# Products with stationary weights: three 256-column matmuls into one accumulator instead of a 512- and a 256-column one that are joined

## The chip, the core and the metric

The kernel runs on one core of one Trainium2 chip. The metric is the device time of one execution in microseconds. TensorE multiplies and writes to accumulators in PSUM; VectorE, ScalarE and GpSimd do the elementwise work; SyncE and ScalarE issue the DMAs. The engines run side by side and wait for one another through semaphores.

## The reference, cut to what matters

One layer of a decoder, for 256 tokens of width 2048, in float32:

```
h   = rmsnorm(x, mix_norm_g)
qkv = h @ w_in                       # 2048 x 6144: 8 + 8 heads of 128, each q, k, v
a   = softmax attention on heads 0-7 (q and k rotated in 32 of 128 dimensions, causal)
b   = stick-breaking attention on heads 8-15 (sigmoids and running products, causal)
x   = x + concat(rmsnorm(a, moba_out_g), rmsnorm(b, sb_out_g)) @ w_out
u   = rmsnorm(x, mlp_norm_g) @ w_up  # 2048 x 8192
x   = x + square(relu(u)) @ w_down   # 8192 x 2048
out = rmsnorm(x, final_norm_g)
```

With 256 tokens there is one block of keys, so the block selection of the first group selects nothing more than its own block.

## The kernel before, in words

Weights of 201 MB are streamed from HBM in 192 items of 1 MiB (512 rows x 512 columns), 48 for q, k and v, 16 for the output projection, 64 for the up and 64 for the down projection. `fetch` (L101) issues an item three items ahead on SyncE's queue into one of three buffers. ScalarE and VectorE split each item into two float32r parts, `wh` (L117, the rounded value) and `wl` (L123, the rest). Activations are split into hi and lo in the same way, and lie side by side in one tile: `actT[:, kt, 0:256]` is hi, `actT[:, kt, 256:512]` is lo. A product is then the sum of three: hi with wh, hi with wl, and lo with wh.

Two forms of product exist. `x_stationary` and `x_part` (L235 to L254) put the tokens on the partitions: activations are loaded as weights of the array, and 512 columns of the weights stream through it, in three matmuls (L242, L243, L244). It serves v, the output and the down projection. `w_stationary` (L218) puts the columns of the weights on the partitions, and the 256 tokens stream: q, k and the up projection, 32 + 64 = 96 items. An item has 4 column blocks (m) and 4 row blocks (k), so 16 steps, and each step of before has two matmuls: L227 loads wh and streams hi and lo, 512 columns, into the two halves of an accumulator; L228 loads wl and streams hi, 256 columns, into the second half. The first half then holds hi*wh, the second hi*wl + lo*wh. Four items (j) complete an accumulation, and at the last step of a block `done(m)` is called.

For q and k, `done` leads to `head_out` (L403) and `qk_out` (L302): ScalarE copies the second half into `low` (L305), VectorE adds the first to it (L306). At a slot of the schedule, `qk_scale` (L308) rotates the first 32 rows if the head is of the first group (L312 to L315, VectorE) and multiplies all by the row scale `r1b` of the first norm (L316, GpSimd). For the up projection, `done` leads to `up_out` (L467): copy of the second half on ScalarE (L471), add on VectorE (L472), maximum with zero times itself (L473), then the split of the result into hi (L474, ScalarE) and lo (L475, GpSimd).

There are six accumulators of 512 columns (`acc`) and two for attention (`att`). A group of q, k or up blocks uses four of the six.

The order of the work on each engine is written out by hand: `step` (L268) runs one item, with the split of the item two ahead woven in, and `at(slot, f)` puts attention and scaling work into slots, two of them in an item. The row scale `r1b` is made at slot 12, in item 6; the first q heads are complete after item 3, the first k heads after item 11.

Of the kernel before, what the change touches and what calls it, by code (L numbers as in the profile page):

```python
# [9 lines left out]
F32 = mybir.dt.float32  # L10
F32R = mybir.dt.float32r
AF = mybir.ActivationFunctionType
ALU = mybir.AluOpType
AX = mybir.AxisListType

P = 128
S = 256
# [6 lines left out]
HALF = 16  # L24
# [7 lines left out]


def shape_constants():
    """What depends on shapes alone: the rotary angles and the causal mask's fill."""
    inv = (THETA ** (-np.arange(HALF, dtype=np.float32) / HALF)).astype(np.float32)
    ang = np.arange(S, dtype=np.float32)[None, :] * inv[:, None]
    c, s = np.cos(ang, dtype=np.float32), np.sin(ang, dtype=np.float32)
    out = np.zeros((P, 2 * S + 3 * P), np.float32)
    out[:2 * HALF, :S] = np.concatenate([c, c])  # L40
    out[:2 * HALF, S:2 * S] = np.concatenate([-s, s])
    diag = np.where(np.arange(P)[None, :] <= np.arange(P)[:, None], 0.0, NEG)
    out[:, 2 * S:2 * S + P] = diag
    out[:, 2 * S + 2 * P:] = diag
    return out
# [3 lines left out]
def layer(ctx: ExitStack, tc, x, mix_g, w_in, moba_g, sb_g, w_out, mlp_g, w_up, w_down, fin_g,  # L49
          consts, out):  # L50
    nc = tc.nc
# [5 lines left out]
    att = pool("att", 2, space=bass.MemoryType.PSUM)  # L57
    ctx.enter_context(tc.manual_schedule())

    # ---- constants and small operands  # L60
    xs = cp.tile([P, 2, D], F32, name="xs")
    xv = x.rearrange("(t p) d -> p t d", p=P)
    grow = cp.tile([2 * HALF, P], F32, name="grow")
# [2 lines left out]
    cosr, sinr, dmask = cst[:32, :S], cst[:32, S:2 * S], cst[:, 2 * S:]  # L66

    def load_x(c):
# [7 lines left out]
                            fill=0.0, base=0, channel_multiplier=1)  # L76
    mhalf = cp.tile([P, 2], F32, name="mhalf")
    nc.gpsimd.memset(mhalf, -0.5)

    # ---- weight stream: 1 MiB items, each split exactly into two float32r parts  # L80
    items = []
    for h in range(2):
        for kind in ("q", "v", "k"):
# [15 lines left out]
    raws, parts = {}, {}  # L99
# [26 lines left out]
        split_hi(i, slice(k, k + n))  # L126
        split_lo(i, slice(k, k + n))

    # ---- row statistics
    def rms_scale(r, ss, n):  # L130
        """r = (ss / n + eps) ** -0.5"""
        nc.vector.tensor_scalar(r, ss, 1.0 / n, EPS, op0=ALU.mult, op1=ALU.add)
        nc.gpsimd.tensor_tensor(r, r, mhalf[:, :r.shape[-1]], op=ALU.pow)

# [2 lines left out]
    actT = cp.tile([P, 16, 2 * S], F32R, name="actT")  # L137

    def to_columns(src, gcol, kts, between=None):
        """Transposes [token, d] into d on the partitions, times gain, in two parts."""  # L140
        ps = [att.tile([P, 512], F32, name="att") for _ in range(2)]
        for n, k in enumerate(kts):
            for t in range(2):
                c = n // 2 * S + t * P
                nc.tensor.transpose(ps[n % 2][:, c:c + P], src[:, t, k * P:(k + 1) * P], ident)  # L145
        for n, k in enumerate(kts):
            g = g48[:, gcol + k:gcol + k + 1]
            src_ps = ps[n % 2][:, n // 2 * S:(n // 2 + 1) * S]
            hi, lo = actT[:, k, 0:S], actT[:, k, S:2 * S]
            nc.scalar.activation(hi, src_ps, AF.Copy, scale=g)  # L150
            nc.vector.scalar_tensor_tensor(lo, src_ps, g, hi.bitcast(F32), op0=ALU.mult, op1=ALU.subtract)  # L151
            if between:
                between(n)
# [9 lines left out]
    r1b = cp.tile([P, S], F32, name="r1b")  # L163

    def x_piece(c, n):
        """A quarter of x, and the split of the weights that meet it, n of its tiles at a time."""
        def between(k):
            if k % 2:
                for j in range(k - 1, k + 1, n):
                    split_k(c, j, n)  # L170

        to_columns(xs, 0, list(range(4 * c, 4 * c + 4)), between)
# [3 lines left out]
            nc.scalar.activation(junk, xs[:, t, c * CW:(c + 1) * CW], AF.Square, accum_out=ss1[:, t, c:c + 1])  # L176

    def x_scale():
        """The first norm's row scale, along the tokens of every partition."""
        nc.vector.tensor_reduce(r1, ss1, axis=AX.X, op=ALU.add)  # L180
        rms_scale(r1, r1, D)
        for t in range(2):
            nc.vector.tensor_scalar(junk[:, t * P:(t + 1) * P], ident, r1[:, t:t + 1], None, op0=ALU.mult)
# [7 lines left out]
    idle = acc.tile([P, 512], F32, name="acc")  # L191

    def warm(n):
        """Products that nobody reads, for the array's clock to rise while the first loads run."""
        for _ in range(n):
            nc.tensor.transpose(idle[:, :P], ident, ident)

# [16 lines left out]
        nc.tensor.transpose(ps[:, :32], grow, ident[:32, :32])  # L214
        nc.vector.tensor_copy(g48[:, 16:48], ps[:, :32])

    # ---- products
    def w_stationary(i, ps, j, nj, done):  # L218
        """Columns of the weights on the partitions: [hi*hi | hi*lo + lo*hi]."""
        wh, wl = parts.pop(i)  # L220
        mk = [(m, k) for m in range(4) for k in range(KI)]
        if i < 3:
            mk = [(m, k) for k in range(KI) for m in range(4)]
        for n, (m, k) in enumerate(mk):
            kt = j * KI + k
            first, last = j == 0 and k == 0, j == nj - 1 and k == KI - 1
            nc.tensor.matmul(ps[m], wh[:, k, m * P:(m + 1) * P], actT[:, kt, :], start=first, stop=False)  # L227
            nc.tensor.matmul(ps[m][:, S:2 * S], wl[:, k, m * P:(m + 1) * P], actT[:, kt, 0:S],  # L228
                             start=False, stop=last)
            if last:  # L230
                done(m)
            if n == (3 if i < 3 else 7):
                yield

    def x_part(i, ps, j, nj, xT, k0, t, done):  # L235
        """Tokens on the partitions."""
        wh, wl = parts[i]
        for k in range(KI):
            kt = k0 + j * KI + k
            first, last = j == 0 and k == 0, j == nj - 1 and k == KI - 1  # L240
            hi, lo = xT[:, kt, t * P:(t + 1) * P], xT[:, kt, S + t * P:S + (t + 1) * P]
            nc.tensor.matmul(ps[t], hi, wh[:, k, :], start=first, stop=False)  # L242
            nc.tensor.matmul(ps[t], hi, wl[:, k, :], start=False, stop=False)  # L243
            nc.tensor.matmul(ps[t], lo, wh[:, k, :], start=False, stop=last)  # L244
        if last:
            done(t)
# [9 lines left out]
    hooks = {}  # L256

    def at(slot, f, *a):
        """Slots are half items: 2 * i in the middle of item i, 2 * i + 1 at its end."""
        hooks.setdefault(slot, []).append((f, a))  # L260

    def run_hooks(slot):
# [3 lines left out]
    state = {"i": 0}  # L266
# [23 lines left out]
    at(10, x_scale)  # L290
    at(12, x_spread)

    # ---- attention
    with ExitStack() as phase:
        qkvp = phase.enter_context(tc.tile_pool(name="qkvp", bufs=2))
        aw = phase.enter_context(tc.tile_pool(name="aw", bufs=2))
# [2 lines left out]
        osq = op.tile([P, S], F32, name="osq")  # L299
        rg = op.tile([P, 2, 2], F32, name="rg")  # L300

        def qk_out(dst, ps, m):  # L302
            """Joins the two accumulators of a head."""
            low = aw.tile([P, S], F32, name="low")
            nc.scalar.copy(low, ps[:, S:2 * S])  # L305
            nc.vector.tensor_add(dst[:, m, :], ps[:, 0:S], low)  # L306

        def qk_scale(dst, m, rope):  # L308
            """Rotates the first 32 rows of a head, and applies the norm's scale."""
            if rope:  # L310
                rot = aw.tile([32, 2, S], F32, name="rot", bufs=1)
                nc.vector.stream_shuffle(rot[:, 0], dst[:32, m, :], [(r + HALF) % 32 for r in range(32)])  # L312
                nc.vector.tensor_mul(rot[:, 0], rot[:, 0], sinr)
                nc.vector.tensor_mul(rot[:, 1], dst[:32, m, :], cosr)
                nc.vector.tensor_add(dst[:32, m, :], rot[:, 0], rot[:, 1])  # L315
            nc.gpsimd.tensor_mul(dst[:, m, :], dst[:, m, :], r1b)  # L316

        def scores(qT, kT, m):
            ps = att.tile([P, 512], F32, name="att")
# [71 lines left out]
        for gi, (g, h) in enumerate(((1, 0), (1, 1), (0, 0), (0, 1))):  # L391
# [10 lines left out]

            def head_out(kind, m):  # L403
                dst = qT if kind == "q" else kT
                qk_out(dst, ps[m], m)
                if kind == "q":
                    at(2 * state["i"] + (6 if gi == 0 else 0) + 2 * m, qk_scale, dst, m, rope)
                elif m == 0:
                    qk_scale(dst, m, rope)
                else:  # L410
                    at(2 * state["i"] + gap * m - 1, qk_scale, dst, m, rope)

            for kind in "qvk":
                ps = [acc.tile([P, 512], F32, name="acc") for _ in range(2 if kind == "v" else 4)]
# [12 lines left out]
            if h == 1:  # L427
                at(i0 + 2 + gap * 3 + d2 + 2, group_scale, g)

        # ---- output projection and residual, one group after the other  # L430
        ssx = op.tile([P, 2, 4], F32, name="ssx")

        def o_out(g, c, ps, t):
# [25 lines left out]

    at(2 * state["i"] + 16, load_fgb)  # L460

    # ---- squared-ReLU MLP, in two halves of its inner width; relu(r u) ** 2 = r * r * relu(u) ** 2
    uT = mp.tile([P, 32, 2 * S], F32R, name="uT")
    ssf = mp.tile([P, 2, 4], F32, name="ssf")
    rf = mp.tile([P, 2], F32, name="rf")

    def up_out(ps, f):  # L467
        low = mw.tile([P, S], F32, name="ulow")
        u = mw.tile([P, S], F32, name="u")
        hi, lo = uT[:, f, 0:S], uT[:, f, S:2 * S]  # L470
        nc.scalar.copy(low, ps[:, S:2 * S])  # L471
        nc.vector.tensor_add(u, ps[:, 0:S], low)  # L472
        nc.vector.scalar_tensor_tensor(u, u, 0.0, u, op0=ALU.max, op1=ALU.mult)  # L473
        nc.scalar.activation(hi, u, AF.Copy)  # L474
        nc.gpsimd.tensor_sub(lo, u, hi.bitcast(F32))  # L475

# [12 lines left out]
                finish(t)  # L489

    def finish(t):
        """The last norm, in quarters that leave as they are ready."""
        r = rf[:, t:t + 1]
        nc.vector.scalar_tensor_tensor(r, ssf[:, t, 3:4], 1.0 / D, r, op0=ALU.mult, op1=ALU.add)
        nc.gpsimd.tensor_tensor(r, r, mhalf[:, :1], op=ALU.pow)
# [51 lines left out]
```

## Time and profile before

| | us |
|---|---|
| median of 3 runs | 1113.27 (1113.21 to 1113.61) |
| span of the profiled execution, first to last instruction | 1111.6 |
| the median beyond that span | 1.7 |
| TensorE matmuls busy | 1099.6 |
| VectorE busy | 632.7 |
| ScalarE busy | 505.7 |
| GpSimd busy | 130.8 |

The profiled execution's own time is shown by its span alone; what lies around the span is taken as the difference to the median. "PE" is TensorE's matmuls, "PEld" its weight loads, "DVE" VectorE, "ACT" ScalarE, "POOL" GpSimd, "SP" SyncE. Matmuls overlap in the pipeline and their ends are modelled, so the mean duration of one is longer than the distance from its start to that of the next.

### The profile page before, as it was taken

Reading aid. Unit: us, or ns where it says so; the run is one execution under the profiler, and the core shown is the slowest. Engines: PE = TensorE matmul, PEld = TensorE weight load, DVE = VectorE, ACT = ScalarE, POOL = GpSimd, SP = SyncE. Lnnn points to the kernel's source line nnn. Section 1 sums busy time; section 2 is a strip of 40 time slices with the busy share of each in tenths; the row PEclk is TensorE's granted clock in tenths of the full one; section 3 lists DMA queues with packets and bytes.
Section 4 is the critical chain, followed back from the end, with each engine's and each line's share of the span. In section 5 each row is a group of like instructions: output and inputs, shape, how many; then the busy total and the mean of one; then the engine's idle time right before and its main releaser. Section 6 shows DMA issues by size and latency. Waiting matters only on the chain.

```text
span 1111.6 us, 14050 instructions
## 1 busy us (share of the span) xinstructions
PE 1099.6 (99%) x5648; PEld 936.8 (84%) x5648; DVE 632.7 (57%) x813; ACT 505.7 (45%) x732; POOL 130.8 (12%) x154
## 2 busy tenths in 40 slices
PE   8999999999999999999999999999999999999997
PEld 7888888888888888888888888888888888888885
DVE  5655657668676665655564444435655665455453
ACT  5645444455444554544453333333544454334341
POOL 0101213223111001211220000000111211000000
PEclk9999999999999999999999999999999999999999
DMA  8655454554444555566546546554565456555542
GB/s 303 233 166 179 160 189 153 189 189 152 172 169 173 183 184 180 191 218 208 178 154 244 197 163 227 189 189 152 197 219 190 152 201 216 189 198 192 203 164 75
DMA packets 104113, 207.96 MB, mean 187 GB/s; under 512 B 3392, under 2 KB 3440, under 8 KB 103920
## 3 DMA queue, kind: packets, MB, share of 16 engines
q1 hardware_dynamic: 103088, 204.49, 53.8%
q10 hardware_dynamic: 960, 2.58, 0.6%
q8 instruction: 44, 0.72, 0.3%
q14 instruction: 21, 0.17, 0.0%
HBM read 204.96 MB, written 2.10 MB: 186 GB/s over the span
## 4 chain that ended last, share of the span: by engine, by line
PE 98%; DMA 1%; issue 1%; DVE 0%; ACT 0%; SPq 0%; POOLq 0%; POOL 0%; DVEq 0%
PE acc L227 32%; PE acc L228 16%; PE acc L242 16%; PE acc L244 16%; PE acc L243 16%; PE att L321 1%; PE att L372 1%; PE att L145 1%; DMA raw<-in_w_in 1%; PE att L362 0%; PE att L373 0%; PE att L320 0%; DVE wl L123 0%; DVE xs L479 0%; ACT junk L482 0%
## 5 line engine op out<-in xcount | busy, mean ns | idle before, releaser
L123 DVE TENSOR_TENSOR wl<-raw,wh 128x1024 fp32r<-128x1024 f32 (+1 forms) x386 | 461.2, 1231 | 197.6 <-ACT wh L117 197.6
L117 ACT ACTIVATE wh<-raw 128x1024 fp32r<-128x1024 f32 (+1 forms) x385 | 389.5, 1051 | 351.7 <-PE acc L244 199.0
L227 PE MATMUL acc<-actT,wh 128*128 128x512 f32 x1536 | 536.6, 393 | 0.6 <-DVE actT L151 0.6
L228 PE MATMUL acc<-actT,wl 128*128 128x256 f32 x1536 | 429.5, 280 | 0.2 <-DVE wl L123 0.2
L227 PEld LDWEIGHTS acc<-actT,wh 128*128 128x128 f32 x1536 | 288.4, 188 | 63.6 <-ACT wh L117 0.8
L228 PEld LDWEIGHTS acc<-actT,wl 128*128 128x128 f32 x1536 | 288.5, 188 | 0.9 <-DVE wl L123 0.5
L242 PE MATMUL acc<-wh,uT 128*128 128x512 f32 x512 | 199.2, 389 | 0.0
L244 PE MATMUL acc<-wh,uT 128*128 128x512 f32 x512 | 199.2, 389 | 0.0
L243 PE MATMUL acc<-wl,uT 128*128 128x512 f32 x512 | 199.2, 389 | 0.0
L475 POOL TENSOR_TENSOR uT<-u,uT 128x256 fp32r<-128x256 f32 x64 | 61.7, 964 | 510.6 <-ACT uT L474 510.6
L244 PEld LDWEIGHTS acc<-wh,uT 128*128 128x128 f32 x512 | 96.1, 188 | 20.1
L243 PEld LDWEIGHTS acc<-wl,uT 128*128 128x128 f32 x512 | 96.1, 188 | 20.0
L242 PEld LDWEIGHTS acc<-wh,uT 128*128 128x128 f32 x512 | 96.1, 188 | 19.7
L472 DVE TENSOR_TENSOR u<-acc,ulow 128x256 f32<-128x256 f32 x64 | 27.2, 425 | 100.0 <-ACT ulow L471 90.2
L474 ACT ACTIVATE uT<-u 128x256 fp32r<-128x256 f32 x64 | 26.8, 418 | 67.0 <-DVE u L473 67.0
L242 PE MATMUL acc<-wh,actT 128*128 128x512 f32 x128 | 53.1, 415 | 0.0
L242 PE MATMUL acc<-wh,oT 128*128 128x512 f32 x128 | 52.2, 408 | 0.0
L243 PE MATMUL acc<-wl,oT 128*128 128x512 f32 x128 | 50.5, 395 | 0.0
L244 PE MATMUL acc<-wh,oT 128*128 128x512 f32 x128 | 50.5, 394 | 0.0
L243 PE MATMUL acc<-wl,actT 128*128 128x512 f32 x128 | 50.4, 394 | 0.0
L244 PE MATMUL acc<-wh,actT 128*128 128x512 f32 x128 | 50.4, 394 | 0.0
L479 DVE SCALAR_TENSOR_TENSOR xs<-acc,r,xs 128x512 f32<-128x512 f32 x16 | 12.0, 750 | 45.3 <-PE acc L244 45.3
(105 smaller groups left out, 572.1 us busy)
## 6 DMA issues: line engine op xcount, KB each, us to landing
raw<-in_w_up SPq DMA_DIRECT2D x64, 1024.0 KB, 6.2
raw<-in_w_down SPq DMA_DIRECT2D x64, 1024.0 KB, 5.0
raw<-in_w_in SPq DMA_DIRECT2D x47, 1024.0 KB, 5.2
raw<-in_w_out SPq DMA_DIRECT2D x16, 1024.0 KB, 5.0
xs<-in_x SPq DMA_DIRECT2D x4, 512.0 KB, 9.6
raw<-in_w_in SPq DMA_DIRECT2D x4, 256.0 KB, 5.9
fgb<-in_final_norm_g ACTq DMA_DIRECT2D x1, 1024.0 KB
out<-xs SPq DMA_DIRECT2D x4, 256.0 KB, 3.2
```

Source lines behind the costliest of these rows:

```text
L117: nc.scalar.activation(parts[i][0][:, ks], raws[i][:, ks], AF.Copy)
L123: nc.vector.tensor_sub(wl[:, ks], raws[i][:, ks], wh[:, ks].bitcast(F32))
L145: nc.tensor.transpose(ps[n % 2][:, c:c + P], src[:, t, k * P:(k + 1) * P], ident)
L227: nc.tensor.matmul(ps[m], wh[:, k, m * P:(m + 1) * P], actT[:, kt, :], start=first, stop=False)
L228: nc.tensor.matmul(ps[m][:, S:2 * S], wl[:, k, m * P:(m + 1) * P], actT[:, kt, 0:S], start=False, stop=last)
L242: nc.tensor.matmul(ps[t], hi, wh[:, k, :], start=first, stop=False)
L243: nc.tensor.matmul(ps[t], hi, wl[:, k, :], start=False, stop=False)
L244: nc.tensor.matmul(ps[t], lo, wh[:, k, :], start=False, stop=last)
L472: nc.vector.tensor_add(u, ps[:, 0:S], low)
L474: nc.scalar.activation(hi, u, AF.Copy)
L475: nc.gpsimd.tensor_sub(lo, u, hi.bitcast(F32))
L479: nc.vector.scalar_tensor_tensor(xs[:, t, cs], ps[t], r2[:, t:t + 1], xs[:, t, cs], op0=ALU.mult, op1=ALU.add)
```

## The change

The three products of a step each become a 256-column matmul into the first half of the accumulator, in the order hi*wh, hi*wl, lo*wh. The second half isn't written any more, and nothing is joined. `qk_out` scales by `r1b` while it reads the accumulator (VectorE), except for the first four q heads, which are copied by ScalarE and scaled later on GpSimd as before; the rotation is a function of its own and now comes after the scaling. `up_out` takes Relu on ScalarE from the accumulator and squares on VectorE.

```diff
@@ w_stationary
-            nc.tensor.matmul(ps[m], wh[:, k, m * P:(m + 1) * P], actT[:, kt, :], start=first, stop=False)
-            nc.tensor.matmul(ps[m][:, S:2 * S], wl[:, k, m * P:(m + 1) * P], actT[:, kt, 0:S],
-                             start=False, stop=last)
+            mc = slice(m * P, (m + 1) * P)
+            nc.tensor.matmul(ps[m][:, :S], wh[:, k, mc], actT[:, kt, 0:S], start=first, stop=False)
+            nc.tensor.matmul(ps[m][:, :S], wl[:, k, mc], actT[:, kt, 0:S], start=False, stop=False)
+            nc.tensor.matmul(ps[m][:, :S], wh[:, k, mc], actT[:, kt, S:2 * S], start=False, stop=last)
@@ qk_out, qk_scale
-        def qk_out(dst, ps, m):
-            low = aw.tile([P, S], F32, name="low")
-            nc.scalar.copy(low, ps[:, S:2 * S])
-            nc.vector.tensor_add(dst[:, m, :], ps[:, 0:S], low)
+        def qk_out(dst, ps, m, scaled):
+            if scaled:
+                nc.vector.tensor_mul(dst[:, m, :], ps[:, 0:S], r1b)
+            else:
+                nc.scalar.copy(dst[:, m, :], ps[:, 0:S])
-        def qk_scale(dst, m, rope):
-            if rope:
...
+        def qk_scale(dst, m):
             nc.gpsimd.tensor_mul(dst[:, m, :], dst[:, m, :], r1b)
+        def qk_rope(dst, m):
...
@@ head_out
-                qk_out(dst, ps[m], m)
-                if kind == "q":
-                    at(2 * state["i"] + (6 if gi == 0 else 0) + 2 * m, qk_scale, dst, m, rope)
-                elif m == 0:
-                    qk_scale(dst, m, rope)
-                else:
-                    at(2 * state["i"] + gap * m - 1, qk_scale, dst, m, rope)
+                early = gi == 0 and kind == "q"
+                qk_out(dst, ps[m], m, not early)
+                if early:
+                    at(2 * state["i"] + 6 + 2 * m, qk_scale, dst, m)
+                if rope:
+                    if kind == "k" and m == 0:
+                        qk_rope(dst, m)
+                    else:
+                        at(2 * state["i"] + (2 * m if kind == "q" else gap * m - 1), qk_rope, dst, m)
@@ up_out
-        low = mw.tile([P, S], F32, name="ulow")
+        a = mw.tile([P, S], F32, name="urelu")
...
-        nc.scalar.copy(low, ps[:, S:2 * S])
-        nc.vector.tensor_add(u, ps[:, 0:S], low)
-        nc.vector.scalar_tensor_tensor(u, u, 0.0, u, op0=ALU.max, op1=ALU.mult)
+        nc.scalar.activation(a, ps[:, 0:S], AF.Relu)
+        nc.vector.tensor_mul(u, a, a)
```

## Rows read from the trace of the kernel before

**Rows 1.** The page, part 1: busy us (share of the span) xinstructions.

```profile
PE 1099.6 (99%) x5648; PEld 936.8 (84%) x5648; DVE 632.7 (57%) x813; ACT 505.7 (45%) x732; POOL 130.8 (12%) x154
```

**Rows 2.** The chain that ended last: by engine, and by line.

```profile
PE 98%; DMA 1%; issue 1%; DVE 0%; ACT 0%; SPq 0%; POOLq 0%; POOL 0%; DVEq 0%
by line: PE acc L227 31.7%; PE acc L228 16.2%; PE acc L242 15.7%; PE acc L244 15.7%; PE acc L243 15.6%; PE att L321 0.6%; PE att L372 0.6%; PE att L145 0.6%; DMA raw<-in_w_in 0.5%; issue 0.5%; PE att L362 0.5%; PE att L373 0.3%; PE att L320
```

**Rows 3.** TensorE's waits, all five: us in total, times, longest.

```profile
PE acc L196 <- POOL mhalf L78: 1.5, 1, 1.5
PE att L145 <- DMA xs<-in_x: 0.8, 1, 0.8
PE att L145 <- DVE wl L123: 0.6, 1, 0.6
PE acc L227 <- DVE actT L151: 0.6, 1, 0.6
PE acc L228 <- DVE wl L123: 0.2, 1, 0.2
```

**Rows 4.** The cores: span and mean granted TensorE clock.

```profile
core 0: 1111.6 us, clock 0.998
```

**Rows 5.** Timeline of PE, up projection: start, us, matmul; ten L227 starts.

```profile
449.87 0.39 PE L227 MATMUL acc<-actT,wh 128*128 128x512 f32 x1
...
452.99 0.39 PE L227 MATMUL acc<-actT,wh 128*128 128x512 f32 x1
```

**Rows 6.** Timeline of PE, down projection: first and last of ten starts.

```profile
599.70 0.39 PE L244 MATMUL acc<-wh,uT 128*128 128x512 f32 x1
...
601.74 0.39 PE L244 MATMUL acc<-wh,uT 128*128 128x512 f32 x1
```

**Rows 7.** Chain in order of time, output projection: first and last of 37.

```profile
379.93 0.23 PE acc L244
...
388.33 0.23 PE acc L244
```

**Rows 8.** The page, part 5: the matmuls of the product, and loads of the first.

```profile
L227 PE MATMUL acc<-actT,wh 128*128 128x512 f32 x1536 | 536.6, 393 | 0.6 <-DVE actT L151 0.6
L228 PE MATMUL acc<-actT,wl 128*128 128x256 f32 x1536 | 429.5, 280 | 0.2 <-DVE wl L123 0.2
L227 PEld LDWEIGHTS acc<-actT,wh 128*128 128x128 f32 x1536 | 288.4, 188 | 63.6 <-ACT wh L117 0.8
```

**Rows 9.** Chain in order of time: the eight transposes of a piece.

```profile
395.56 0.87 PE att L145 x8
```

**Rows 10.** Timeline of PE around the score products of one head.

```profile
87.53 0.28 PE L228 MATMUL acc<-actT,wl 128*128 128x256 f32 x1
87.64 0.38 PE L320 MATMUL att<-kT,qT 128*128 128x128 f32 x2
87.86 0.60 PE L321 MATMUL att<-kT,qT 128*128 128x256 f32 x2
...
88.53 0.28 PE L228 MATMUL acc<-actT,wl 128*128 128x256 f32 x1
```

**Rows 11.** Groups by line and form: xcount | busy us, mean ns | idle before.

```profile
L305 ACT COPY low<-acc 128x256 f32<-128x256 f32 x32 | 11.6, 372 | 13.9 <-PE acc L228 13.7
L316 POOL TENSOR_TENSOR qT<-qT,r1b 128x256 f32<-128x256 f32 x16 | 21.8, 1371 | 30.6 <-DVE qT L315 25.3 <-ACT r1b L189 5.4
L316 POOL TENSOR_TENSOR kT<-kT,r1b 128x256 f32<-128x256 f32 x16 | 20.0, 1248 | 73.0 <-DVE kT L315 48.4 <-DVE kT L306 24.6
L471 ACT COPY ulow<-acc 128x256 f32<-128x256 f32 x64 | 23.0, 359 | 7.1 <-PE acc L228 7.1
L472 DVE TENSOR_TENSOR u<-acc,ulow 128x256 f32<-128x256 f32 x64 | 27.2, 425 | 100.0 <-ACT ulow L471 90.2 <-POOL uT L475 9.9
L473 DVE SCALAR_TENSOR_TENSOR u<-u 128x256 f32<-128x256 f32 x64 | 27.2, 426 | 2.2
L474 ACT ACTIVATE uT<-u 128x256 fp32r<-128x256 f32 x64 | 26.8, 418 | 67.0 <-DVE u L473 67.0
```

More of the change, by code (lines that the diff above doesn't have):

```diff
@@ L300, in layer @@
         rg = op.tile([P, 2, 2], F32, name="rg")
-        def qk_out(dst, ps, m):
-            low = aw.tile([P, S], F32, name="low")
-            nc.scalar.copy(low, ps[:, S:2 * S])
-            nc.vector.tensor_add(dst[:, m, :], ps[:, 0:S], low)
-        def qk_scale(dst, m, rope):
-            if rope:
[L311 to L315, printed above, removed]
-            nc.gpsimd.tensor_mul(dst[:, m, :], dst[:, m, :], r1b)
+        def qk_out(dst, ps, m, scaled):
[4 more added lines that the diff above has]
+        def qk_scale(dst, m):
+            nc.gpsimd.tensor_mul(dst[:, m, :], dst[:, m, :], r1b)
+        def qk_rope(dst, m):
+            rot = aw.tile([32, 2, S], F32, name="rot", bufs=1)
+            nc.vector.stream_shuffle(rot[:, 0], dst[:32, m, :], [(r + HALF) % 32 for r in range(32)])
+            nc.vector.tensor_mul(rot[:, 0], rot[:, 0], sinr)
+            nc.vector.tensor_mul(rot[:, 1], dst[:32, m, :], cosr)
+            nc.vector.tensor_add(dst[:32, m, :], rot[:, 0], rot[:, 1])
         def scores(qT, kT, m):
```

## The prediction

> **What bounds the kernel now.** I read the busy shares first [rows 1]: TensorE is busy 1099.6 of 1111.6 us, the other engines 57% and less. A busy share alone proves little here, because the ends of matmuls are modelled, so I went on to the chain of waits [rows 2]. There the reader is to see that the chain that ended last lies 98% on TensorE, and that the two lines of the product with stationary weights hold 31.7% (L227, 512 columns) and 16.2% (L228, 256 columns) of it. Third, TensorE's own waits [rows 3]: five entries, each met once, 1.5 + 0.8 + 0.6 + 0.6 + 0.2 = 3.7 us in the whole span, all in the first microseconds. No vector, scalar or DMA work is late for TensorE after that. So a microsecond taken from VectorE or ScalarE is worth nothing, and what counts is the distance from one matmul's start to the next one's. I call it a slot.
>
> The mean granted clock is 0.998 of full speed [rows 4], the 2.4 GHz level. Reckoned at one column per cycle, 256 columns take 106.7 ns and 512 take 213.3 ns. The slots are longer:
> - In the product with stationary weights 9 pairs take 452.99 - 449.87 = 3.12 us, so 346.7 ns for one pair [rows 5]. Its 768 columns account for 320.0; 26.7 ns are excess.
> - In the down projection, 512 columns each time, 9 slots take 601.74 - 599.70 = 2.04 us: 226.7 ns each, excess 13.3 [rows 6].
> - In the output projection 36 slots take 388.33 - 379.93 = 8.40 us: 233.3 ns each, excess 20 [rows 7].
>
> How a pair splits is read from the chain: 31.7% of 1111.6 us over 1536 matmuls [rows 2, 8] is 229.4 ns for the 512-column slot, and 16.2% is 180.1 us, 117.2 ns for the 256-column slot. The sum, 346.6 ns, agrees with the starts.
>
> **The change part by part.**
>
> *The matmuls.* Each of the 1536 steps (96 items of 16 steps: 32 items of q and k, 64 of the up projection) before issues a 512- and a 256-column matmul, each with its own weight load [rows 8]. After the change there are three of 256, with loads of wh, wl and wh again, since wl stands between the two uses of wh. The columns stay 768; 1536 matmuls and 1536 loads are added. The price depends on whether the excess goes with instructions or with columns, and no row shows 256-column slots one after another. I take the slot nearest to it, the 256-column one with a 128x128 load behind it: 117.2 ns. Three make 351.6 ns, 4.9 to 5.0 ns more than the pair. Over all steps: 3 x 180.1 - (352.4 + 180.1) = **+7.7 us**. All of it is on the path, as nothing else is waited for there.
>
> Bounds of this term. Below: eight 128-column transposes, each with a load, run in 0.87 us, a slot of 109 ns [rows 9]. A slot cannot be thought much shorter, as 106.7 ns are columns. Three times 109 is 327 ns: 19.7 ns less than a pair, -30 us. Above: the largest steady excess that the trace shows is the 20 ns of the output projection; 3 x 126.7 = 380 ns, 33.3 more, +51 us. I stay at the 117.2, because it is the same matmul form, with the same weights and the same moving tile, 1536 times.
>
> A fixed cost of an instruction can be read in one more place. Between two L228 starts, 87.53 and 88.53 [rows 10], there lie one pair (346.7) and two score products, each of two instructions; so 653 ns are left for four instructions. The two of 128 columns start 0.22 us before the next, thus 110 ns each; read as two cycles a column. Two of 106.7 and two of 213.3 are 640: 13 ns over for four instructions, 3.3 each. With 3.3 ns for each added instruction the sum would be 1536 x 3.3 = +5.1 us. This is a rival below. The Trainium skill has such a rule (TensorE: Matmul & The Clock Gate, Back-to-back issue gap): an isolated matmul of N columns takes N / 2.4 ns and 2.5 ns on top at the full clock. By it the 1536 extra instructions would cost 3.8 us, an estimate from that page. The slots in rows 6 carry 13.3 ns on top, so this trace does not bear it out for this form.
>
> *Vector and scalar work.* Gone are the copies of the second accumulator on ScalarE (32 x 372 and 64 x 359 ns), the joining adds on VectorE (32 and 64 x 425) and 28 of the 32 row-scale products on GpSimd (1248 to 1371 ns each) [rows 11]. New are 64 Relu reads on ScalarE in place of those 64 copies, a plain square on VectorE in place of the max-and-multiply (64 x 426), 28 products with the row scale on VectorE in place of adds, and 4 copies on ScalarE for the first q heads, whose scale is not there yet. I price new forms like the rows of the same shape, 359 to 425 ns. Net: about 10 us less on ScalarE, 29 us less on VectorE, 37 us less on GpSimd. All of it lies beside TensorE, whose waits for it are nil in these stages [rows 3]; worth 0. If the cover were gone, a wait could appear only where a new group of four accumulators waits for old ones, and one chain of copy, add, multiply and split, 359 + 425 + 426 + 418 ns, shows what that would be: under 2 us a group, while two of the six accumulators are free beforehand. The accumulator is now released by the first reader, so earlier than before.
>
> *The rotation* is split from the scale. It stays at the same slots of the schedule, on VectorE, and ahead of the scores as before; no DMA is issued in it and no queue is passed. The first keys' scale now comes straight at the end of item 11, and the row scale it reads is made at item 6. Nothing.
>
> *The start.* In the first items TensorE waits some of its 3.7 us [rows 3]. The third matmul of a step can only fill such time: under 0.3 us. I count 0.
>
> **The sum.** Span 1111.6 + 7.7 = 1119.3 us. The median of the runs, 1113.27, lies 1.7 us above the profiled span; with the same 1.7 the time is **1121.0 us**, +0.7%. With a slot of 116.7 to 118.4 ns, which is about what stamps of 0.01 us leave open, the pair grows by 3.4 to 8.5 ns and the time by 5 to 13 us: the forecast's own range is 1118 to 1126.
>
> **The rivals.**
> 1. *The excess belongs to the instruction* (chance 0.18). The down projection has 13.3 ns for one instruction, the pair 26.7 for two: exactly twice. Then 3 x (106.7 + 13.3) = 360 ns, +13.3 ns, +20.5 us: 1133.8. For it: how neatly the two numbers fit. Against it: the chain gives the 512-column slot of the pair 229.4, not 226.7, and the output projection has 20 for one instruction.
> 2. *The excess belongs to the columns, a small part to the instruction* (0.10): 3.3 ns for each added instruction, +5.1 us, 1118.4. For it: rows 10. Against it: three stages with three excesses for the same columns.
> 3. *Faster: the 256-column slot falls to the pace of the loads* (0.09). Place: every step of the 96 items. If the 10 ns of excess in a 256-column slot come from the change between unequal lengths, three equal matmuls settle at the 109 ns of the transposes: -30 us, 1083; half of that effect gives 1098. It decides below 346.7 / 3 = 115.6 ns a slot. For it: rows 9 have load and matmul in 109 ns. Against it: those come eight at a time, and no 256-column slot of this form is that short.
> 4. *No change* (0.08): the excess is of the columns alone, 26.7 ns in 768 whatever their division, 1113.3. It needs that the load costs nothing; the different excess in rows 6 and 7 at equal shape leaves room for that.
> 5. *Issue or loads become the bound* (0.06). Now four instructions are issued in 346.7 ns; then six in about 352, 59 ns each, and without a pause; the trace shows such a pace only in bursts like rows 9. If the slot is drawn out to 126.7 ns, the excess of rows 7, the cost is +51 us: 1164.
>
> The forecast itself has the remaining 0.49.
>
> **How the numbers follow.** A measurement of this kernel can tell a change from none at about 0.2%, 2.2 us. Slower are the forecast, rivals 1, 2 and 5: 0.83; a little of rival 2 lies near the edge, so 0.81. Faster is rival 3 with a bit of 4: 0.10. The same: 0.09. The range that leaves out rivals 3 and 5 and some of 4 runs from 1112 to 1135.
>
> **What would show it right or wrong.** TensorE should show 5648 + 1536 = 7184 matmuls, as many loads, waits as short as now and a chain still about 98% on it. The starts in the up projection decide the rest: steps of 350 to 355 ns for the forecast, 360 for rival 1, 347 for rival 4, 330 to 340 for rival 3, 370 and more for rival 5. The slots of the other products must stay at 226.7 and 233.3. I am wrong in kind if TensorE waits for ScalarE's Relu or for a DMA, or if a step takes under 346.7 ns.

## The result, and the profile after

The changed kernel takes 1127.18 us (median of 4 runs, 1126.03 to 1127.23) against 1113.44 us (4 runs): the ratio is 1.0121, 95% interval 1.0107 to 1.0136, so 13.7 us slower. The span grew from 1111.6 to 1125.5 us, by 13.9.

The page of the changed kernel, part 1, and its chain by line, are read first (L228, L229 and L230 are the three matmuls of a step; L243 to L245 are the three of the other form):

```profile
PE 1114.6 (99%) x7184; PEld 1015.9 (90%) x7184; DVE 607.9 (54%) x745; ACT 501.0 (45%) x704; POOL 92.7 (8%) x126
PE 98%; issue 0%; DMA 0%; DVE 0%; ACT 0%; POOLq 0%; POOL 0%; DVEq 0%
by line: PE acc L229 16.2%; PE acc L228 16.2%; PE acc L230 16.2%; PE acc L243 15.5%; PE acc L244 15.5%; PE acc L245 15.4%; PE att L145 0.7%; PE att L324 0.6%; PE att L375 0.6%; PE att L365 0.5%; issue 0.5%; DMA xs<-in_x 0.4%; PE att L323 0.
```

Matmuls and loads grew by 1536 each, to 7184. VectorE is busy 24.8 us less, ScalarE 4.7, GpSimd 38.1 [rows 1], and none of that appears in the time: the chain still lies 98% on TensorE [rows 2]. Its waits are now two, both at the start (us in total, times, longest), against five before [rows 3]:

```profile
PE acc L196 <- POOL mhalf L78: 1.5, 1, 1.5
PE att L145 <- DMA xs<-in_x: 0.6, 1, 0.6
```

The granted clock is that of before [rows 4]:

```profile
core 0: 1125.5 us, clock 0.998
```

The loss must then lie in the slots. The timeline of TensorE in the up projection, first columns start and modelled duration in us:

```profile
449.91 0.28 PE L228 MATMUL acc<-actT,wh 128*128 128x256 f32 x1
450.02 0.28 PE L229 MATMUL acc<-actT,wl 128*128 128x256 f32 x1
450.14 0.28 PE L230 MATMUL acc<-actT,wh 128*128 128x256 f32 x1
450.26 0.28 PE L228 MATMUL acc<-actT,wh 128*128 128x256 f32 x1
...
452.76 0.28 PE L228 MATMUL acc<-actT,wh 128*128 128x256 f32 x1
```

Between the first row and the last lie eight steps, 2.85 us or 356 ns each, 118.7 ns a slot. The pair before took 346.7 [rows 5], 9.3 ns less. The whole first half of the up projection agrees. From its first matmul to the first of the down projection, the kernel before and then the changed one:

```profile
399.07 0.39 PE L227 MATMUL acc<-actT,wh 128*128 128x512 f32 x1
...
577.44 0.40 PE L242 MATMUL acc<-wh,uT 128*128 128x512 f32 x1
```

```profile
403.13 0.28 PE L228 MATMUL acc<-actT,wh 128*128 128x256 f32 x1
...
586.26 0.40 PE L243 MATMUL acc<-wh,uT 128*128 128x512 f32 x1
```

That is 178.37 us before and 183.13 after: 4.76 more for 512 steps. The second half grew by 4.78. The 9.3 ns do not hold for all 1536 steps, though. The stages of q and k, taken from start to start in the same way, grew by 3.5 us in their 512 steps, 6.9 ns each. So the steps make 13.0 of the 13.9 us. Of the rest, 0.56 lies ahead of the first product, which starts at 8.21 us and not at 7.65, and 0.36 behind the second up projection.

Why q and k lose less can be seen in the changed kernel's own timeline. A long unbroken stretch of steps keeps one of two paces. This one, in the product for q, takes 29 steps in 10.21 us, 352 ns a step or 117.4 a slot:

```profile
164.70 0.28 PE L228 MATMUL acc<-actT,wh 128*128 128x256 f32 x1
...
174.91 0.28 PE L228 MATMUL acc<-actT,wh 128*128 128x256 f32 x1
```

Other stretches of q and k take 356. In the up projection the first steps run at 352, until the last transposes come between at 405.95 us; from there on, and in all of the second half, it is 356. What chooses the pace is not shown.

The down projection has not changed: in 8 groups of three from 620.26 on it takes 5.44 us, 226.7 ns a slot, as in rows 6.

```profile
620.26 0.39 PE L243 MATMUL acc<-wh,uT 128*128 128x512 f32 x1
...
625.70 0.39 PE L243 MATMUL acc<-wh,uT 128*128 128x512 f32 x1
```

### The profile page after: what moved, and what is told of

Same layout as the page of the kernel before. It is cut to its first block, busy times and chain, and to the rows that moved or that the text cites. A ratio compares the mean times of both kernels' runs of the same rounds, so it can differ in the third digit from the quotient of the medians.

```text
span 1125.5 us, 16976 instructions
## 1 busy us (share of the span) xinstructions
PE 1114.6 (99%) x7184; PEld 1015.9 (90%) x7184; DVE 607.9 (54%) x745; ACT 501.0 (45%) x704; POOL 92.7 (8%) x126
## 4 chain that ended last, share of the span: by engine, by line
PE 98%; issue 0%; DMA 0%; DVE 0%; ACT 0%; POOLq 0%; POOL 0%; DVEq 0%
PE acc L229 16%; PE acc L228 16%; PE acc L230 16%; PE acc L243 15%; PE acc L244 15%; PE acc L245 15%; PE att L145 1%; PE att L324 1%; PE att L375 1%; PE att L365 0%; DMA xs<-in_x 0%; PE att L323 0%; PE att L376 0%; ACT actT L150 0%; DVE xs L483 0%
## 5 line engine op out<-in xcount | busy, mean ns | idle before, releaser
L228 PE MATMUL acc<-actT,wh 128*128 128x256 f32 x1536 | 434.2, 283 | 0.0
L229 PE MATMUL acc<-actT,wl 128*128 128x256 f32 x1536 | 431.6, 281 | 0.1
L230 PE MATMUL acc<-actT,wh 128*128 128x256 f32 x1536 | 431.4, 281 | 0.0
L229 PEld LDWEIGHTS acc<-actT,wl 128*128 128x128 f32 x1536 | 290.0, 189 | 0.7 <-DVE wl L123 0.4
L228 PEld LDWEIGHTS acc<-actT,wh 128*128 128x128 f32 x1536 | 290.0, 189 | 0.5 <-ACT wh L117 0.2
L230 PEld LDWEIGHTS acc<-actT,wh 128*128 128x128 f32 x1536 | 289.9, 189 | 0.0
L243 PE MATMUL acc<-wh,uT 128*128 128x512 f32 x512 | 199.2, 389 | 0.0
L245 PE MATMUL acc<-wh,uT 128*128 128x512 f32 x512 | 199.2, 389 | 0.0
L243 PEld LDWEIGHTS acc<-wh,uT 128*128 128x128 f32 x512 | 96.1, 188 | 20.1
L245 PEld LDWEIGHTS acc<-wh,uT 128*128 128x128 f32 x512 | 96.1, 188 | 19.9
L477 DVE TENSOR_TENSOR u<-urelu 128x256 f32<-128x256 f32 x64 | 34.2, 535 | 104.9 <-ACT urelu L476 95.3
L243 PE MATMUL acc<-wh,actT 128*128 128x512 f32 x128 | 53.0, 414 | 0.0
L243 PE MATMUL acc<-wh,oT 128*128 128x512 f32 x128 | 52.3, 408 | 0.0
L245 PE MATMUL acc<-wh,actT 128*128 128x512 f32 x128 | 50.5, 395 | 0.0
L245 PE MATMUL acc<-wh,oT 128*128 128x512 f32 x128 | 50.5, 395 | 0.0
```

Of the source, the lines that this page charges most:

```text
L228: nc.tensor.matmul(ps[m][:, :S], wh[:, k, mc], actT[:, kt, 0:S], start=first, stop=False)
L229: nc.tensor.matmul(ps[m][:, :S], wl[:, k, mc], actT[:, kt, 0:S], start=False, stop=False)
L230: nc.tensor.matmul(ps[m][:, :S], wh[:, k, mc], actT[:, kt, S:2 * S], start=False, stop=last)
L477: nc.vector.tensor_mul(u, a, a)
```

## The experiments

My theory after the result: the matmul with its load that is added in every step makes all of the difference. The rivals: the accumulation thrice into the same columns; the new vector work; the second load of wh right after another weight; a load too long for a 256-column slot; traffic of the other engines in SBUF. The steps below are all from the up projection, between the two rows shown, unless the text says another stage.

**The split alone.**

```diff
-  matmul(ps[m], wh[:, k, mc], actT[:, kt, :], ...)
+  matmul(ps[m][:, :S], wh[:, k, mc], actT[:, kt, 0:S], ...)
+  matmul(ps[m][:, S:2 * S], wh[:, k, mc], actT[:, kt, S:2 * S], ...)
   matmul(ps[m][:, S:2 * S], wl[:, k, mc], actT[:, kt, 0:S], ...)     # and the kernel before's joining
```

> The kernel before with its 512-column matmul cut into two of 256 columns (wh with hi into the first half of the accumulator, wh with lo into the second), wl with hi into the second half as before, and the joining and scaling of before. If the added instruction with its load is the cost, the step takes 356 ns as in the changed kernel (there 8 steps took 2.85 us) and the time is 1113.4 + 1536 x 9.4 ns = 1128 us (1126 to 1130). If the cost comes from three matmuls into the same 256 columns, or from the new vector work, the step stays at 347 ns and the time at 1113 to 1115 us.

Measured 1126.83 us, ratio 1.0123 (1.0109 to 1.0137). Timeline:

```profile
449.92 0.28 PE L227 MATMUL acc<-actT,wh 128*128 128x256 f32 x1
...
452.77 0.28 PE L227 MATMUL acc<-actT,wh 128*128 128x256 f32 x1
```

Eight steps in 2.85 us, as in the changed kernel. The added matmul with its load is the cause; where the products accumulate and who reads them out is not.

**The evacuation alone**, that is, the work that reads the accumulators out.

```diff
   # the changed kernel, with
-  three 256-column matmuls into ps[m][:, :S]
+  matmul(ps[m], wh[:, k, mc], actT[:, kt, :], ...)
+  matmul(ps[m][:, S:2 * S], wl[:, k, mc], actT[:, kt, 0:S], ...)
```

> The changed kernel with the matmuls of before (512 and 256 columns), and its own evacuation, which reads the first half of the accumulator only: the sum of the two cross products is left out of the result, and no work replaces it. It shows the vector side of the change alone. If that is worth nothing, 1113.4 us within 2 us and 347 ns a step. If lighter vector work gives something that the matmuls then took away, under 1111 us; if the Relu and the products from the accumulator cost something, 1116 us and more.

Measured 1113.25 us, ratio 1.0002 (0.9993 to 1.0011), and eight steps in 2.77 us:

```profile
449.73 0.39 PE L228 MATMUL acc<-actT,wh 128*128 128x512 f32 x1
...
452.50 0.39 PE L228 MATMUL acc<-actT,wh 128*128 128x512 f32 x1
```

The page of this run has the other engines' work as in the changed kernel:

```profile
PE 1099.6 (99%) x5648; PEld 936.7 (84%) x5648; DVE 608.2 (55%) x745; ACT 500.6 (45%) x704; POOL 92.6 (8%) x126
```

The vector side of the change is worth nothing that could be measured, in either direction.

**The order.** The two matmuls with wh follow each other.

```diff
   matmul(ps[m][:, :S], wh[:, k, mc], actT[:, kt, 0:S], ...)
-  matmul(ps[m][:, :S], wl[:, k, mc], actT[:, kt, 0:S], ...)
   matmul(ps[m][:, :S], wh[:, k, mc], actT[:, kt, S:2 * S], ...)
+  matmul(ps[m][:, :S], wl[:, k, mc], actT[:, kt, 0:S], ...)
```

> The changed kernel with the order wh with hi, wh with lo, wl with hi, so that the two matmuls with the same weights follow each other. If every matmul pays for its own load whatever was loaded before, nothing changes: 356 ns a step, 1127 us (1126 to 1128). If a load of the same weights is cheaper, or the change of weights is what costs, one slot in three falls to 109 to 110 ns: 347 ns a step and 1113 us.

Measured 1126.51 us, ratio 1.012 (1.0106 to 1.0134), and eight steps in 2.85 us:

```profile
449.68 0.28 PE L228 MATMUL acc<-actT,wh 128*128 128x256 f32 x1
...
452.53 0.28 PE L228 MATMUL acc<-actT,wh 128*128 128x256 f32 x1
```

A load of the weights that are there already is no cheaper.

**Two matmuls of 512 columns, and four of 256.** Both add wl with lo to the result, so they compute the same.

```diff
   # first kernel: the kernel before, with
-  matmul(ps[m][:, S:2 * S], wl[:, k, mc], actT[:, kt, 0:S], ...)
+  matmul(ps[m], wl[:, k, mc], actT[:, kt, :], ...)
   # second kernel: the changed one, and after its three
+  matmul(ps[m][:, :S], wl[:, k, mc], actT[:, kt, S:2 * S], ...)
```

> The kernel before with wl also streaming hi and lo, so two matmuls of 512 columns a step (the product of the two small parts is added to the result). The step gives the 512-column slot in this very place, which the pair of before does not show alone. If a matmul costs its columns and 13.3 ns, 453 ns a step and 1113.4 + 1536 x 106.7 ns = 1277 us. If its slot is the 229.4 ns that the chain of the kernel before puts down to L227, 459 ns and 1286 us. If it is the 233.3 ns of the output projection, 467 ns and 1298 us.

> The changed kernel with a fourth 256-column matmul in each step (wl with lo, the product of the two small parts, is added). It computes what the run with two 512-column matmuls a step computed, 468.7 ns a step there. If a 256-column slot is 118.7 ns whatever stands beside it, 475 ns a step, 1127 + 1536 x 118.7 ns = 1309 us, so two instructions more for the same columns cost only 6 ns. If an added instruction costs the 9.4 ns that it cost from two to three, 468.7 + 18.8 = 487.5 ns and 1329 us.

Measured 1300.49 and 1305.19 us (one run each). The first kernel, then the second in the first half of the up projection, then the second in its other half:

```profile
519.94 0.40 PE L227 MATMUL acc<-actT,wh 128*128 128x512 f32 x1
...
523.69 0.40 PE L227 MATMUL acc<-actT,wh 128*128 128x512 f32 x1
```

```profile
519.93 0.28 PE L228 MATMUL acc<-actT,wh 128*128 128x256 f32 x1
...
523.68 0.28 PE L228 MATMUL acc<-actT,wh 128*128 128x256 f32 x1
...
960.13 0.28 PE L228 MATMUL acc<-actT,wh 128*128 128x256 f32 x1
...
969.62 0.28 PE L228 MATMUL acc<-actT,wh 128*128 128x256 f32 x1
```

Two 512-column matmuls take 3.75 / 8 = 469 ns, 234.4 a slot. Four of 256 take 469 ns as well in the first half (117.2 a slot), and 9.49 / 20 = 474.5 ns in the other (118.6). So two more instructions cost 0 to 6 ns for the same 1024 columns, not twice 9.3; and here too one line of code has two paces in one run.

The 512-column slot is 234.4 ns here, near the 233.3 of the output projection [rows 7] and not the 229.4 that the chain of the kernel before shows. Slots with their own kind would make a pair of 234.4 + 118.7 = 353.1 ns, or 351.6 with the quicker 117.2. The pair of before takes 346.7, so it is 5 to 6 ns better than its parts. In these terms most of the 9.3 ns is a favourable combination that was lost. This is bookkeeping at one place of `actT`, not a cause that a run shows.

**Half loads**, in the changed kernel and in the one before.

```diff
+  q = P if first or last else 64
-  mc = slice(m * P, (m + 1) * P)
+  mc = slice(m * P, m * P + q)
-  matmul(ps[m][...], wh[:, k, mc], ...)
+  matmul(ps[m][:q, ...], wh[:, k, mc], ...)      # and the others of the step alike
```

> The changed kernel with weight loads of 64 columns instead of 128 in 14 of 16 steps of an accumulation (the lower half of each block's rows is then left out of those sums). The moving side keeps its 256 columns. If the load behind a matmul sets the 256-column slot (118.7 ns against 106.7 of columns), the step falls from 356 towards 320 to 333 ns in those steps and the time by 0.875 x 1536 x 23 to 36 ns = 31 to 48 us, to 1079 to 1096. If the excess belongs to the matmul instruction itself, the step stays at 356 ns and the time at 1127 us.

> The kernel before (512 and 256 columns) with weight loads of 64 columns in 14 of 16 steps (the lower half of each block's rows is left out of those sums). In the changed kernel halving the loads took the step from 356 to 351.3 ns. If loads cost there because three of them follow each other behind short matmuls, the pair stays at 346.7 ns here and the time at 1113 us. If each load costs 1.6 ns wherever it stands, the pair falls by 3.2 ns, 1109 us.

Measured 1120.50 and 1114.35 us (one run each). The changed kernel with half loads, then the kernel before with them:

```profile
479.84 0.28 PE L229 MATMUL acc<-actT,wh 128*64 128x256 f32 x1
...
482.65 0.28 PE L229 MATMUL acc<-actT,wh 128*64 128x256 f32 x1
```

```profile
449.77 0.39 PE L229 MATMUL acc<-actT,wh 128*64 128x512 f32 x1
...
452.55 0.39 PE L229 MATMUL acc<-actT,wh 128*64 128x512 f32 x1
```

2.81 and 2.78 us for eight: 351 and 347 ns. The first kernel's time lies between the two that were expected. The load does not set the slot: halved, it gives 4.7 ns of three slots' 36 ns excess back in the step of three, and nothing in the pair. The edit halves more than the load, namely the columns of the array in use and the rows written to PSUM, so the 4.7 ns cannot be put down to the load alone. 351 ns is also close to the 352 that full loads have at their quicker pace.

**Quiet neighbours.** 62 of the 64 items of the up projection use the parts of the first of their half; in the second kernel they are not fetched either.

```diff
+  def kept(i): return items[i][0] == "u" and items[i - 1][0] == "u"
   # split_hi, split_lo (second kernel: fetch too)
+  if kept(i): ...  # no work; parts[i] are those of the first item
```

> The changed kernel in which the up projection uses the two parts of its first item again and again, so that ScalarE and VectorE split no weights there (62 of 64 items are left out of the split; the DMAs go on). If the excess of 36 ns a step comes from reads of SBUF that ScalarE and VectorE disturb, the step falls in the up projection, to 330 to 350 ns, and the time by 1024 x 6 to 26 ns, 6 to 27 us. If it belongs to instruction and load, 356 ns and 1127 us.

> As the run with quiet vector engines, and the 62 items are not loaded from HBM either, so that in the up projection TensorE has SBUF nearly to itself. If DMA writes disturb the reads, the step falls below that of the run with quiet vector engines. If the excess belongs to instruction and load, 356 ns again and 1127 us.

Measured 1126.96 and 1126.31 us (one run each). Busy time and DMA in one stretch of the up projection, for the changed kernel and for the second of the two (columns: PE, PEld, DVE, ACT, POOL, granted clock, DMA share, GB/s):

```profile
420.00:540.00 120.00, 120.00 (x1014) 120.00 (x1013) 60.23 (x63) 57.72 (x86) 20.67 (x22) 1.00 0.59 194
```

```profile
420.00:540.00 120.00, 120.00 (x1014) 120.00 (x1013) 13.83 (x23) 17.06 (x46) 16.31 (x22) 1.00 0.03 10
```

VectorE falls from 60 to 14 us, DMA from 194 to 10 GB/s, and TensorE has 1014 matmuls on record in both. The second kernel's step is still 356 ns, ten in 3.56 us:

```profile
480.14 0.28 PE L238 MATMUL acc<-actT,wh 128*128 128x256 f32 x1
...
483.70 0.28 PE L238 MATMUL acc<-actT,wh 128*128 128x256 f32 x1
```

The excess of the step of three is not caused by the other engines' traffic.

**No zeros in the down projection.**

```diff
-  nc.scalar.activation(a, ps[:, 0:S], AF.Relu)
+  nc.scalar.activation(a, ps[:, 0:S], AF.Copy)
```

> The changed kernel with a plain copy in place of the Relu, so that the activations of the down projection have no zeros (the Relu is left out of the result). It asks why the same 512-column matmuls take 226.7 ns in the down projection and 233.3 ns in the output projection. If zeros in the array are the reason, the down projection rises to 233 ns a slot, 1536 x 6.7 = +10 us, 1137 us. If place or stage is the reason, 226.7 ns and 1127 us.

Measured 1125.83 us (one run). From L243 at 620.25 to 625.69, 24 slots take 5.44 us: 226.7 ns, unchanged. Zeros are not why the down projection is quicker.

**The place of a tile.** In SBUF the rows of `wh`, `wl` and `uT` begin at the same offset modulo 2048 bytes, counted from the sizes of the tiles; those of `actT` and `oT` begin at others. The move shifts `actT` by 1120 bytes, to the offset of `wh`, and only four small tiles change place with it.

```diff
+  ss1 = cp.tile(...); r1 = cp.tile(...); r1b = cp.tile(...); r2 = cp.tile(...)   # moved up from below
   actT = cp.tile([P, 16, 2 * S], F32R, name="actT")
```

> The kernel before with the activations' tile actT moved by 1120 bytes in SBUF (four small tiles are allocated ahead of it), so that its rows start at the same offset modulo 2048 bytes as those of wh, wl and uT; nothing else moves. The slots of the down projection are 226.7 ns with uT at that offset, those of v and of the output projection 233.3 with actT and oT at others. If the offset between the loaded and the streamed tile is the reason, v falls to 226.7 ns (the output projection stays), and the pair of the product with stationary weights may fall from 346.7 by up to 6.7 x 1.5 ns; the time is then 1098 to 1111 us. If place has nothing to do with it, 1113 us.

> The changed kernel with the same move of actT. If the offset between the loaded and the streamed tile makes part of a slot's excess, v falls to 226.7 ns and the step of three falls from 356 ns, to 346 or 351, 1112 to 1120 us. If it has nothing to do with it, 1127 us and 356 ns.

Measured 1120.84 us, ratio 1.0067 (1.0053 to 1.008), for the kernel before with the move, and 1131.82 us, ratio 1.0167 (1.0153 to 1.0181) to the kernel before, for the changed one with it: 7.7 us (medians) above the kernel before, 4.6 above the changed one. The product for v in the kernel before, and with the move; below that the pair with the move, and the step of three with it:

```profile
117.40 0.40 PE L242 MATMUL acc<-wh,actT 128*128 128x512 f32 x1
...
120.90 0.40 PE L242 MATMUL acc<-wh,actT 128*128 128x512 f32 x1
```

```profile
118.16 0.39 PE L243 MATMUL acc<-wh,actT 128*128 128x512 f32 x1
...
121.56 0.39 PE L243 MATMUL acc<-wh,actT 128*128 128x512 f32 x1
...
449.94 0.40 PE L228 MATMUL acc<-actT,wh 128*128 128x512 f32 x1
...
471.14 0.40 PE L228 MATMUL acc<-actT,wh 128*128 128x512 f32 x1
```

```profile
450.00 0.28 PE L229 MATMUL acc<-actT,wh 128*128 128x256 f32 x1
...
452.88 0.28 PE L229 MATMUL acc<-actT,wh 128*128 128x256 f32 x1
```

Both times fell in none of the ranges expected. Half of the expectation came true: v fell from 233.3 ns (15 slots in 3.50 us) to 226.7 (3.40 us). But the pair rose from 346.7 to 353.3 ns (60 pairs in 21.20 us) and the step of three from 356 to 360. That 353.3 is near the 353.1 reckoned above proves nothing: those parts were measured without the move, and with it a 256-column slot in a row takes 120.0. Place in SBUF is worth more than half as much as the whole change, with opposite sign for the two forms of product. With the move, the third instruction costs 360.0 - 353.3 = 6.7 ns instead of 9.3.

## Why the prediction was right, and where its size was not

- *The bound.* Right. The chain stayed 98% on TensorE, and 68 us less of vector, scalar and GpSimd work left the ratio at 1.0002 in the run that had it alone. Of the savings forecast, 29 us on VectorE and 10 on ScalarE came out at 24.8 and 4.7 (the square of the changed kernel, for one, takes 535 ns where 425 had been priced); beside TensorE that cost nothing.
- *The matmul term.* Right in kind and sign, too small in size: forecast +7.7 us (its own terms add up to 7.8), measured +13.0 in the steps. The step that was mis-sized is "the slot nearest to it, the 256-column one with a 128x128 load behind it: 117.2 ns". Three in a row have that slot only at the quicker of their two paces, in part of q and k. In nearly all of the up projection, two thirds of the steps, the slot takes 118.7. The split of a pair into 229.4 and 117.2, read from the chain, is no property of the two matmuls: with its own kind the longer one takes 234.4, and at another place of `actT` the pair takes 353.3 ns.
- *The number.* The range of 1112 to 1135 held the time; the forecast's own 1118 to 1126 missed it by 1.2 us. The up projection's 356 ns lies between the sign set for the forecast, 350 to 355, and that of rival 1, 360, and the time about midway between their 1121.0 and 1133.8. The time alone does not choose between the two; the runs with 1024 columns a step do, against rival 1.
- *Rival 1*, 13.3 ns for each instruction, 1133.8 us: wrong as a law. By it two 512-column matmuls would take 453 ns and four of 256 would take 480; measured are 469, and 469 to 475. With the moved tile the step takes just its 360 ns, but the pair then takes 353.3, not the 346.7 that the rule was read from.
- *Rival 2*, 3.3 ns for an added instruction, 1118.4 us: too little. Here the third instruction costs 5.3 ns at the quicker pace and 9.3 at the slower. The Trainium skill gives 2.5 ns on top of the columns for an isolated matmul (TensorE: Matmul & The Clock Gate, Back-to-back issue gap); the slot of 118.7 ns is 12 ns above its columns here.
- *Rival 3*, a slot that falls to the transposes' 109 ns, was to be decided below 115.6 ns: it fell, with 117.4 to 118.7 ns for three equal matmuls. Loads of half the length do not bring it about either, at 117.1.
- *Rival 4*, no change: fell, with 352 to 356 ns a step and not 346.7. Yet where 1024 columns were cut into two or four, the step stayed at 469 ns in half of the up projection, so the excess does not always go with the instructions.
- *Rival 5*, issue as the bound, fell: a slot of 118.7 ns and not 126.7, and four matmuls with their four loads in the 469 ns of two with two.
- *Vector work and rotation at nothing.* Right. *The start*, forecast at nothing to under 0.3 us better, came 0.56 us later in this trace; in the traces of the other runs the first product starts anywhere from 7.4 to 8.9 us, so this is not put down to the change.

What stays open: why a 256-column slot takes 117.2, 118.7 or 120 ns, what chooses the pace of a stretch, and why a 512-column slot takes 226.7, 229 or 234. For the step of three the runs exclude the other engines' traffic, DMA, the order of weights and the accumulator; for the down projection, zeros. No run adds a matmul without its load, or a load alone, so the price of the added pair is not divided between them. The runs show that the place of a tile changes the slot, and for three in a row the half loads with what they halve besides. Which property of the address counts cannot be separated from two places alone. A place that favours both forms, or a move of `oT`, was not tried, and no version here beats the kernel before.

## What to carry to other kernels

Where TensorE is never late, price a change by the distance between starts, and take a matmul's slot from a stretch of its own kind: the shares of a mixed pair are not the prices of its members. Read it over whole stages, too, since one form had two paces here and eight steps show only one of them. Cutting one matmul into two cost 5 to 9 ns in each of 1536 steps, while the vector work beside a saturated TensorE cost nothing; so keep the longer matmul and pay for the join elsewhere. And before two forms of a product are compared, see whether tiles have changed place in SBUF: a move of 1120 bytes was worth 0.7%.

## What was not expected of the hardware

- The place of the streamed or loaded tile in SBUF: v 233.3 to 226.7 ns a slot, the pair 346.7 to 353.3, the step of three 356 to 360, by a move of 1120 bytes (four small tiles moved with it).
- The same code has two paces in one run: three 256-column matmuls in 352 or 356 ns, four of them in 469 ns in the first half of the up projection and 474.5 in the second. A long stretch keeps its pace; it mostly changes where another product has come between.
- After an interruption v, with its tile moved, does not run at 226.7 ns a slot at once: groups of three start at 116.68, 117.46, 118.16 and 118.84 us, so the first two take 0.78 and 0.70 us and the third 0.68.
